# Five taps of each convolution tile on TensorE, and the sink's logit as a score column, in a two-layer decoder trunk

## The chip, the cores and the metric

The kernel runs on one core of one Trainium2 chip. The metric is the device time of one execution in microseconds (us), as a median over several runs. TensorE (PE in the profile) has a clock that is granted at one of two levels, 2.4 or 1.2 GHz; the profile gives it as a share of the higher one.

## The reference

512 tokens of 1024 channels pass two layers and a final RMS norm. The change lies in layer 0's mixer alone. It has two branches over one normalised input:

```python
q, k, v, glu = jnp.split(proj, [A_Q, A_Q + A_KV, A_Q + 2 * A_KV], axis=-1)
a, _ = band_attention(q, k, v, A_WINDOW - 1, sinks)      # 8 heads, window 128
g_a, g_b = jnp.split(glu, 2, axis=-1)
c = g_a * jax.nn.sigmoid(g_b)
c = causal_depthwise_conv(c, conv_w, conv_b)              # 31 taps, 512 channels
c = jax.nn.silu(layer_norm(c, ln_g, ln_b))
return jnp.einsum('bse,ed->bsd', jnp.concatenate([a, c], axis=-1), w_out)
```

In the attention a learned logit per head (the sink) is added to each softmax denominator, with no value behind it:

```python
m = jnp.maximum(jnp.max(s, axis=-1), sink_b)
p = jnp.exp(s - m[..., None])
l = jnp.sum(p, axis=-1) + jnp.exp(sink_b - m)
```

After the mixer stand a SwiGLU layer, layer 1 (dilated attention and a gated unit) and a second SwiGLU layer, all untouched by the change.

## The kernel before

Activations are kept transposed: a tile has 128 channels (or tokens) on the partitions and 512 tokens (or channels) in the free dimension. A product with weights is made of three matmuls on rounded halves (`acc3`, lines 197 to 204: high by high, high by low, low by high); eight of these, over the eight input tiles, make one projection tile. The weights come by DMA in blocks (tile `raw`); ACT rounds them (`w_hi`, L174), and in this stage POOL makes the rest (`w_lo`, L151).

Layer 0's mixer is planned as a list of steps (`C0["steps"]`): `g0` to `g3` are the two projection tiles of one convolution tile each (`a` and `b`), `v`, `k`, `q0` to `q3` the projections of the attention, `S0` to `S3` the scores and `V0` to `V3` the values of two heads each, `A`, `X`, `B`, `Y`, `C` parts of the output projection and `L` the layer norm behind the convolution. TensorE's own order is exactly the order in which the program is written (`manual_schedule`): a planner (`Seq`) counts estimated time, and between two `acc3` it lets the side lines (scores, values, layer norm) put in their matmuls when their planned wait is over. The orders of the other engines are set by a scheduler at build time. Every engine carries out its instructions strictly in its order, so an instruction that waits holds up all behind it.

One convolution tile j has 128 channels. `glu` (L494) makes the padded input `cp` on DVE and ACT. `conv_tile` (L467) splits the 31 taps: ACT makes the scaled copies `prod` (L478; the first one, L475, begins `yc`) and POOL adds them into `yc` (L479); the rest are done by DVE as a chain of multiply-adds in PSUM bank 6 (first tap L481, then L483), and L484 adds the bank to `yc`. Bank 6 is one buffer, so the chains of the four tiles follow each other. `taps=(8, 15, 15, 10)` are the taps of the ACT and POOL part; DVE has 23, 16, 16 and 21. DVE's taps have a low priority (`LATER`), so the scheduler fills them in between other DVE work.

`conv_norm` (L633) turns each finished `yc` on TensorE (L641, into bank 7), takes statistics on DVE (L643) and a copy on ACT (L644); after the fourth tile come the norm (L650 to L662), the turn back (L668) and the activation. `scores0` (L572) makes the scores of two heads in two halves on TensorE (L590, L591); DVE scales, masks and takes the maximum (L598), ACT makes the exponentials and their sums `l` (L610). The sink is treated apart: `es` (L605, L612), its sum with `l` (L614) and the reciprocal (L615). `pt_av` (L399) turns the probabilities (L407, copies `pts` on ACT, L410), multiplies them with the values (L421), scales by the reciprocal on DVE (`on`, L430) and turns the result back (L435). `rope` (L386) is the rotary embedding of q and k.

Of the kernel before, what the change touches and what calls it, by code (L numbers as in the profile page):

```python
# [10 lines left out]
def _warn_once_fixed(msg, *args, **kwargs):  # L11
# [7 lines left out]
F32 = mybir.dt.float32  # L19
# [4 lines left out]
P = 128  # L24
# [18 lines left out]
    taps=(8, 15, 15, 10),  # L43
# [91 lines left out]
def trunk_kernel(ctx: ExitStack, tc: tile.TileContext, xT, ws, cols, sinks, sgu_g, sgu_b,  # L135
# [308 lines left out]
    with ExitStack() as mx:  # L444
# [17 lines left out]
        mp.tile([P, 8, 2 * P], F32, name="Pm", bufs=2)  # L462
# [4 lines left out]
        def conv_tile(j, pool_taps):  # L467

            with tc.high_priority(offset=LATER):
                acc = bank(6)  # L470
                for t in range(TAPS):
# [4 lines left out]
                    elif t < pool_taps:  # L476
                        p = mp.tile([P, S], F32, name="prod", bufs=3)
                        A.activation(p, src, AF.Copy, scale=w)  # L478
                        G.tensor_add(yc[j], yc[j], p)  # L479
                    elif t == pool_taps:  # L480
                        V.tensor_scalar(out=acc, in0=src, scalar1=w, scalar2=None, op0=ALU.mult)  # L481
                    else:
                        V.scalar_tensor_tensor(acc, src, w, acc, op0=ALU.mult, op1=ALU.add)  # L483
                V.tensor_add(yc[j], yc[j], acc)  # L484

# [87 lines left out]
        def scores0(i):  # L573
# [3 lines left out]
            qss = qTs[i][1]  # L577
            Pm = mp.tile([P, 8, 2 * P], F32, name="Pm", bufs=2)
            nm = scr.tile([P, 8], F32, name="nm")
            l = scr.tile([P, 8], F32, name="l")  # L580
            for n2 in range(2):
# [10 lines left out]
                for n1 in range(2):  # L592
                    n = 2 * n2 + n1
                    for b in range(2):
# [4 lines left out]
                            out=Pm[:, u, c0:], in0=sb[b][:, n1 * 256 + c0:n1 * 256 + 256],  # L599
                            in1=mask0[:, c0:], scale=-0.125, scalar=nsink[:, hd:hd + 1],  # L600
                            op0=ALU.add, op1=ALU.min, accum_out=nm[:, u:u + 1])
                if n2 == 0:
                    yield 0.9, C0["S"]
            es = scr.tile([P, 8], F32, name="es")
            V.tensor_tensor(out=es.rearrange("p (n b) -> p n b", b=2),  # L605
                            in0=nm.rearrange("p (n b) -> p n b", b=2),
                            in1=sinkb[:, i:i + 5:4][:, None, :].to_broadcast([P, NQ, 2]), op=ALU.add)
# [4 lines left out]
            A.activation(es, es, AF.Exp)  # L612
            rl = scr.tile([P, 8], F32, name="rl")
            V.tensor_add(rl, l, es)  # L614
            V.reciprocal(rl, rl)  # L615
# [4 lines left out]
        def values0(i):  # L620
# [5 lines left out]
            for u in range(8):  # L626
# [3 lines left out]
                items.append((u, Pm[:, u, P:], n, n == 0, True))  # L630
            yield from pt_av(items, lambda u, blk: Vt[:, blk, 64 * (u % 2):64 * (u % 2) + 64], rl, i, (4, 7))

        def conv_norm():  # L633
# [47 lines left out]
        for step in C0["steps"].split():  # L681
            kind, i = step[0], int(step[1:] or 0)
            if kind == "g":
                pa, pb = gemm_in(f"a{i}"), gemm_in(f"b{i}")

                def after(i=i, pa=pa, pb=pb):
                    glu(i, pa, pb)
                    conv_tile(i, C0["taps"][i])
# [17 lines left out]
            elif kind == "q":  # L706
                ps = gemm_in(step)
                seq.until(lambda: len(qTs) < 2)
                qTs[i] = (mp.tile([P, S], F32, name="qT", bufs=3),
                          [mp.tile([P, S], F32R, name=f"qs{b}", bufs=2) for b in range(2)])  # L710

                def after(i=i, ps=ps, step=step):
                    qT, qss = qTs[i]
# [18 lines left out]
            elif kind == "Y":  # L732
# [4 lines left out]
                early[i] = mp.tile([P, S], F32, name="qT", bufs=3)  # L737
# [603 lines left out]
```

## Time and profile before

| | us |
|---|---|
| median of 3 runs (1117.32, 1123.54, 1124.16) | 1123.54 |
| the profiled execution | 1121.61 |
| its span in the profile | 1119.9 |

The profiled execution's own time is 1.71 us above its span. All durations below come from that one execution. Layer 0's mixer takes the first 208 us of the span; in the first 30 us of them the norm and the first two projection tiles are made. Times in a trace row are from the span's start. A matmul's end is modelled in the records, so the time that a matmul takes of TensorE is read from the distance between starts.

### The profile page before, as it was taken

The numbers are of one execution on the slowest core, as the hardware profiler recorded it, in microseconds if no ns is written. First come the engines' busy times: TensorE is split into PE (matmuls) and PEld (weight loads), VectorE is DVE, ScalarE is ACT, GpSimd is POOL, SyncE is SP. The second block draws the span as 40 slices with busy tenths as digits, with TensorE's granted clock in tenths as the row PEclk, the third lists the DMA queues.
The fourth block names the chain that finished last, engine by engine and source line by source line (L and its number), as shares of the span: only waits on it lengthen the run. The fifth ranks groups of instructions, "written<-read, shape, count | busy, mean of one in ns | idle before, by whom it ended". The sixth has DMA issues, their size and how long they took to land.

```text
span 1119.9 us, 13693 instructions
## 1 busy us (share of the span) xinstructions
PE 1071.8 (96%) x5118; PEld 887.8 (79%) x5118; DVE 693.8 (62%) x1059; ACT 572.9 (51%) x930; POOL 232.8 (21%) x210
## 2 busy tenths in 40 slices
PE   9988789989999999999999999999899999999997
PEld 7767677868788888888887888888688888888785
DVE  3889965777455655654748546666765646555543
ACT  6577756754435343543636654446544453535433
POOL 0789754201101010100014300001111010101002
PEclk9989999999999999999999999999999999999999
DMA  6221112977767677621432111239777676767122
GB/s 230 68 70 57 38 38 75 263 208 190 168 187 150 188 136 217 135 57 50 149 103 76 57 39 58 94 117 237 210 187 179 164 171 180 154 189 150 26 69 76
DMA packets 42803, 145.89 MB, mean 130 GB/s; under 512 B 4848, under 2 KB 5744, under 8 KB 42736
## 3 DMA queue, kind: packets, MB, share of 16 engines
q1 hardware_dynamic: 31072, 102.97, 27.0%
q0 software_dynamic: 11520, 41.95, 22.2%
q8 instruction: 40, 0.66, 0.2%
q14 instruction: 27, 0.22, 0.1%
q10 hardware_dynamic: 144, 0.09, 0.0%
HBM read 142.89 MB, written 2.10 MB: 129 GB/s over the span
## 4 chain that ended last, share of the span: by engine, by line
PE 75%; DVE 9%; DMA 4%; ACT 4%; issue 4%; POOL 3%; POOLq 0%; ACTq 0%; SPq 0%; DVEq 0%
PE bank L201 11%; PE bank L202 10%; PE bank L203 10%; PE bank L904 10%; PE bank L907 10%; PE bank L906 10%; DMA raw<-in_ws 4%; PE bank L262 2%; PE bank L264 2%; PE bank L263 2%; DVE bank L483 2%; PE bank L919 1%; PE bank L421 1%; ACT w2h L880 1%; POOL yc L479 1%
## 5 line engine op out<-in xcount | busy, mean ns | idle before, releaser
L151 DVE TENSOR_TENSOR w2l<-raw,w2h 128x1024 fp32r<-128x1024 f32 x140 | 171.4, 1225 | 206.0 <-ACT w2h L880 206.0
L880 ACT ACTIVATE w2h<-raw 128x1024 fp32r<-128x1024 f32 x140 | 148.0, 1058 | 208.8 <-PE bank L907 159.5
L174 ACT ACTIVATE w_hi<-raw 128x512 fp32r<-128x512 f32 x204 | 127.4, 628 | 180.5 <-PE bank L202 143.4
L870 POOL DMA_DIRECT2D raw<-in_ws x80 | 69.6, 870 | 557.7 <-DVE w2l L151 231.7
L151 DVE TENSOR_TENSOR w_lo<-raw,w_hi 128x512 fp32r<-128x512 f32 x164 | 115.6, 709 | 57.7 <-ACT w_hi L174 57.7
L907 PE MATMUL bank<-w2h,s 128*128 128x512 f32 x320 | 126.0, 394 | 4.3 <-DVE s L151 4.3
L904 PE MATMUL bank<-w2h,s 128*128 128x512 f32 x320 | 126.5, 395 | 2.5 <-ACT s L823 1.4
L906 PE MATMUL bank<-w2l,s 128*128 128x512 f32 x320 | 125.5, 392 | 0.0
L201 PE MATMUL bank<-xh,w_hi 128*128 128x512 f32 x272 | 111.4, 410 | 1.3 <-ACT w_hi L174 1.3
L203 PE MATMUL bank<-xh,w_lo 128*128 128x512 f32 x272 | 108.0, 397 | 0.0
L202 PE MATMUL bank<-xl,w_hi 128*128 128x512 f32 x272 | 107.9, 397 | 0.0
L201 PE MATMUL bank<-hh,w_hi 128*128 128x512 f32 x256 | 100.1, 391 | 1.1 <-DVE hl L151 1.1
L202 PE MATMUL bank<-hl,w_hi 128*128 128x512 f32 x256 | 100.0, 391 | 0.0
L203 PE MATMUL bank<-hh,w_lo 128*128 128x512 f32 x256 | 99.9, 390 | 0.0
L904 PE MATMUL bank<-w2h,xh 128*128 128x512 f32 x240 | 94.4, 393 | 0.0
L907 PE MATMUL bank<-w2h,xl 128*128 128x512 f32 x240 | 93.5, 389 | 0.0
L906 PE MATMUL bank<-w2l,xh 128*128 128x512 f32 x240 | 93.4, 389 | 0.0
L907 PEld LDWEIGHTS bank<-w2h,s 128*128 128x128 f32 x320 | 60.7, 190 | 17.9 <-DVE s L151 5.2
L904 PEld LDWEIGHTS bank<-w2h,s 128*128 128x128 f32 x320 | 60.6, 190 | 16.4 <-ACT s L823 2.3
L906 PEld LDWEIGHTS bank<-w2l,s 128*128 128x128 f32 x320 | 60.5, 189 | 12.4
L151 POOL TENSOR_TENSOR w_lo<-raw,w_hi 128x512 fp32r<-128x512 f32 x40 | 54.6, 1366 | 60.2 <-ACT w_hi L174 57.6
L479 POOL TENSOR_TENSOR yc<-yc,prod 128x512 f32<-128x512 f32 x44 | 60.7, 1381 | 10.5 <-ACT prod L478 9.0
(237 smaller groups left out, 2051.8 us busy)
## 6 DMA issues: line engine op xcount, KB each, us to landing
raw<-in_ws SPq DMA_DIRECT2D x181, 512.0 KB, 4.2
raw<-in_ws POOLq DMA_DIRECT2D x80, 512.0 KB, 5.7
h<-in_xT SPq DMA_DIRECT2D x8, 256.0 KB, 4.8
out_y<-xh SPq DMA_DIRECT2D x4, 256.0 KB, 2.0
out_y<-xl SPq DMA_DIRECT2D x4, 256.0 KB, 2.3
raw<-in_ws SPq DMA_DIRECT2D x2, 256.0 KB, 3.9
ropeC<-in_rope_c SPq DMA_DIRECT2D x2, 256.0 KB, 4.1
ropeS<-in_rope_s SPq DMA_DIRECT2D x2, 256.0 KB, 4.7
```

The lines of the kernel that those rows point to most:

```text
L151: eng.tensor_tensor(out=out, in0=a, in1=b, op=ALU.subtract)
L174: A.activation(hi, src, AF.Copy)
L201: T.matmul(ps, hi, xh, start=start, stop=False)
L202: T.matmul(ps, hi, xl, start=False, stop=False)
L203: T.matmul(ps, lo, xh, start=False, stop=stop)
L262: T.matmul(ps[t], xh[:, c], hi, start=(k == 0), stop=False)
L479: G.tensor_add(yc[j], yc[j], p)
L870: nc.gpsimd.dma_start(t, ws[base + 8 * (g - 1) + 2 * BLOCK_OF[more] + q], accum_op=ALU.add)
L880: A.activation(hi, src, AF.Copy)
L904: T.matmul(ps[t], xh[:, c], wh[:, w], start=(start and j == 0), stop=False, skip_group_check=True)
L906: T.matmul(ps[t], xh[:, c], wl[:, w], start=False, stop=False, skip_group_check=True)
L907: T.matmul(ps[t], xl[:, c], wh[:, w], start=False, stop=(j == 3), skip_group_check=True)
```

## The change

Five taps of each convolution tile leave the chains of ACT, POOL and DVE and become matmuls: ACT scales the identity matrix by a tap's weight column (tile `dg`, a diagonal matrix of 128x128), and TensorE multiplies it with the shifted input `cp`, in float32, five of them accumulated into bank 6. DVE's chain then goes on in that bank with the taps that are left and has no first tap (the former L481) of its own. The taps are now 7, 13, 13, 8 on ACT and POOL, 5, 5, 5, 5 on TensorE and 19, 13, 13, 18 on DVE. The matmuls are a new side line `T` of the planner, with planned times `cv`. The layer norm's planned times `ln` stay, but it does not turn a tile before that tile's five matmuls have been put in.

The scores tile `Pm` gets a 257th column per head and block, which ACT fills with the sink's logit, and the exponential with its sum runs over 257 (or 129) columns. `es`, its exponential and its addition go; the reciprocal is taken from `l`. A q tile's rotary result moves from a tile of its own (`qT`) to the scratch tile `gb`, and the early output sums move to `prod`.

```diff
-    taps=(8, 15, 15, 10),
+    taps=(7, 13, 13, 8), pe_taps=(5, 5, 5, 5),
+    cv=(0.0, 52.0, 67.0, 94.0),
...
-        def conv_tile(j, pool_taps):
+        def conv_tile(j):
             with tc.high_priority(offset=LATER):
-                acc = bank(6)
-                for t in range(TAPS):
+                for t in range(C0["taps"][j]):
...
-                    elif t < pool_taps:
+                    else:
                         p = mp.tile([P, S], F32, name="prod", bufs=3)
                         A.activation(p, src, AF.Copy, scale=w)
                         G.tensor_add(yc[j], yc[j], p)
-                    elif t == pool_taps:
-                        V.tensor_scalar(out=acc, in0=src, scalar1=w, scalar2=None, op0=ALU.mult)
-                    else:
-                        V.scalar_tensor_tensor(acc, src, w, acc, op0=ALU.mult, op1=ALU.add)
+
+        def conv_psum(j):
+            n0, n1 = C0["taps"][j], C0["taps"][j] + C0["pe_taps"][j]
+            yield 0.0, max(1.6, C0["cv"][j] - seq.t)
+            acc = bank(6)
+            for t in range(n0, n1):
+                dg = mp.tile([P, P], F32, name="dg", bufs=6)
+                A.activation(dg, ident, AF.Copy, scale=col("conv_w", j * TAPS + t))
+                T.matmul(acc, dg, cp[j][:, t:t + S], start=(t == n0), stop=(t == n1 - 1))
+            with tc.high_priority(offset=LATER):
+                for t in range(n1, TAPS):
+                    V.scalar_tensor_tensor(acc, cp[j][:, t:t + S], col("conv_w", j * TAPS + t), acc,
+                                           op0=ALU.mult, op1=ALU.add)
                 V.tensor_add(yc[j], yc[j], acc)
+            done.add(("T", j))
+            yield 0.9 * (n1 - n0), 0.0
...
-            Pm = mp.tile([P, 8, 2 * P], F32, name="Pm", bufs=2)
+            Pm = mp.tile([P, 8, 2 * P + 1], F32, name="Pm", bufs=2)
+            A.activation(Pm[:, :, 2 * P:].rearrange("p (n b) o -> p n (b o)", b=2),
+                         nsink[:, i:i + 5:4][:, None, :].to_broadcast([P, NQ, 2]), AF.Copy)
...
-            es = scr.tile([P, 8], F32, name="es")
-            V.tensor_tensor(out=es.rearrange("p (n b) -> p n b", b=2),
-                            in0=nm.rearrange("p (n b) -> p n b", b=2),
-                            in1=sinkb[:, i:i + 5:4][:, None, :].to_broadcast([P, NQ, 2]), op=ALU.add)
...
-            A.activation(es, es, AF.Exp)
             rl = scr.tile([P, 8], F32, name="rl")
-            V.tensor_add(rl, l, es)
-            V.reciprocal(rl, rl)
+            V.reciprocal(rl, l)
...
                 yield 0.0, max(0.0, C0["ln"][j] - seq.t)
+                while ("T", j) not in done:
+                    yield 0.0, 0.3
```

The orders below are those of the built programs. L489 is the new matmul, L492 the taps and L494 the last addition of DVE's chain, L652 the turn of `yc` (L641 before), L436 the turn of `on` (L435 before), L605 and L606 the scores (L590 and L591 before), L613 the masking on DVE (L598 before). Bank names with the same number are one buffer's use.

TensorE, before, where the fourth convolution tile (`yc_139`) is turned: behind the last turn of `on` and eleven `acc3` of the output projection.

```order
L435 MATMUL bank_1509<-ident,on 128x128 x4
L201 MATMUL bank_1516<-oh_312,w_hi 128x512
L202 MATMUL bank_1516<-ol_320,w_hi 128x512
L203 MATMUL bank_1516<-oh_312,w_lo 128x512
...
L201 MATMUL bank_1559<-oh_313,w_hi 128x512
L202 MATMUL bank_1559<-ol_321,w_hi 128x512
L203 MATMUL bank_1559<-oh_313,w_lo 128x512
L641 MATMUL bank_1572<-ident,yc_139 128x128 x4
```

TensorE, now, the same turn: it stands between the third `on` and the two `acc3` behind the fourth tile's five products, ahead of the second half of `S3` (the row with `bank_1480`) and of all of `V3`.

```order
L489 MATMUL bank_1363<-cp_127,dg 128x512 x5
L422 MATMUL bank_1333<-Vt,pts 128x64 x4
L408 MATMUL bank_1402<-ident,Pm 128x128 x2
...
L422 MATMUL bank_1333<-Vt,pts 128x64 x6
...
L204 MATMUL bank_1348<-oh_312,w_lo 128x512
L652 MATMUL bank_1439<-ident,yc_139 128x128 x4
L436 MATMUL bank_1449<-ident,on 128x128 x4
L202 MATMUL bank_1323<-oh_314,w_hi 128x512
L203 MATMUL bank_1323<-ol_322,w_hi 128x512
L204 MATMUL bank_1323<-oh_314,w_lo 128x512
L605 MATMUL bank_1480<-khh_305,qs_1110 128x256
```

The turn moved up, past the last quarter of the scores, the whole of `V3` and nine of the eleven `acc3`.

VectorE, now, the fourth tile's chain (`bank_1363`) from its input `cp_127` to the statistics of its turn:

```order
L514 SCALAR_TENSOR_TENSOR cp_127<-gb,ga 128x512
L492 SCALAR_TENSOR_TENSOR bank_1363<-cp_127,cc,bank_1363 128x512 x3
L613 ISA Pm,nm<-bank_1411,mask_114,nsink 128x128
...
L492 SCALAR_TENSOR_TENSOR bank_1363<-cp_127,cc,bank_1363 128x512
L431 TENSOR_TENSOR on<-bank_1333,rl 128x512
L492 SCALAR_TENSOR_TENSOR bank_1363<-cp_127,cc,bank_1363 128x512 x14
L494 TENSOR_TENSOR yc_139<-yc_139,bank_1363 128x512
L654 BN_STATS bs<-bank_1439 128x6 x4
L661 BN_AGGR mv_1458<-bs 128x2 x4
L663 TENSOR_SCALAR ve_1463<-mv_1458 128x4
```

VectorE, before, the same chain (`bank_1280`), with the first half of `S3` and the second half in the middle of it:

```order
L502 SCALAR_TENSOR_TENSOR cp_127<-gb,ga 128x512
L481 TENSOR_SCALAR bank_1280<-cp_127,cc 128x512
L483 SCALAR_TENSOR_TENSOR bank_1280<-cp_127,cc,bank_1280 128x512 x10
L430 TENSOR_TENSOR on<-bank_1341,rl 128x512
L483 SCALAR_TENSOR_TENSOR bank_1280<-cp_127,cc,bank_1280 128x512 x2
L598 ISA Pm,nm<-bank_1404,mask_114,nsink 128x128
...
L483 SCALAR_TENSOR_TENSOR bank_1280<-cp_127,cc,bank_1280 128x512
L484 TENSOR_TENSOR yc_139<-yc_139,bank_1280 128x512
L430 TENSOR_TENSOR on<-bank_1466,rl 128x512
```

The second half of `S3` and the last `on` moved from inside or right behind the chain to behind the statistics and the norm.

## Rows read from the trace of the kernel before

**Rows 1.** Busy us (x instructions) by stretch: PE, PEld, DVE, ACT, POOL; PEclk, DMA

```profile
30.00:150.00 120.00, 100.69 (x530) 83.37 (x529) 111.73 (x214) 82.84 (x176) 98.28 (x73) 0.96 0.16 53
67.00:68.00 1.00, 0.01 (x1) 0.01 (x1) 0.97 (x2) 1.00 (x1) 1.00 (x2) 0.50 0.00 0
```

**Rows 2.** What TensorE waits for, 33 to 160 us: us in total, times, longest

```profile
PE bank L435 <- DVE on L430: 7.1, 4, 3.5
PE bank L407 <- ACT yn L644: 3.8, 2, 2.8
PE bank L591 <- DVE kl L698: 3.8, 2, 2.5
PE bank L421 <- ACT pts L410: 2.1, 3, 1.3
PE bank L201 <- DVE gb L498: 1.3, 1, 1.3
PE bank L565 <- DVE ga L704: 1.1, 1, 1.1
...
PE bank L590 <- ACT khh L697: 0.5, 1, 0.5
```

**Rows 3.** Groups by line, 30 to 160 us: xcount | busy us, mean ns | idle before

```profile
L483 DVE SCALAR_TENSOR_TENSOR bank<-cp,cc,bank 128x512 f32<-128x512 f32 x72 | 54.1, 751 | 1.2
L598 DVE CUSTOM_DVE_ANT_0 Pm<-bank,mask,nsink 128x256 f32<-128x256 f32 x24 | 10.6, 479 | 0.7 <-PE bank L591 0.7
L605 DVE TENSOR_TENSOR es<-nm,sinkb 128x8 f32<-128x8 f32 x4 | 3.7, 925 | 0.0
L614 DVE TENSOR_TENSOR rl<-l,es 128x8 f32<-128x8 f32 x4 | 2.4, 599 | 0.3 <-ACT es L612 0.3
L610 ACT ACTIVATE Pm<-Pm,nm 128x256 f32<-128x256 f32 x24 | 12.0, 500 | 2.5 <-DVE nm L598 2.5
L479 POOL TENSOR_TENSOR yc<-yc,prod 128x512 f32<-128x512 f32 x44 | 60.7, 1381 | 10.5 <-ACT prod L478 9.0
```

**Rows 4.** TensorE in order of time: start us, us, instruction xcount [idle before <-releaser]

```profile
1.32 4.43 PE L306 MATMUL bank<-sq 128*128 128x256 f32 x10 [1.32 <-DVE sq L303]
29.59 1.05 PE L356 MATMUL bank<-ident,rc 128*128 128x128 f32 x8
30.39 0.48 PE L201 MATMUL bank<-xh,w_hi 128*128 128x512 f32 x1
67.99 0.48 PE L591 MATMUL bank<-kl,qs 128*128 128x128 f32 x1 [2.47 <-DVE kl L698]
69.22 0.63 PE L201 MATMUL bank<-xh,w_hi 128*128 128x512 f32 x1
74.75 0.28 PE L590 MATMUL bank<-khh,qs 128*128 128x256 f32 x1
140.54 0.66 PE L435 MATMUL bank<-ident,on 128*128 128x128 f32 x4 [1.48 <-DVE on L430]
154.10 0.66 PE L435 MATMUL bank<-ident,on 128*128 128x128 f32 x4 [1.24 <-DVE on L430]
208.40 0.95 PE L341 MATMUL bank<-ones,nacc 128*128 128x1 f32 x8
```

**Rows 5.** VectorE in order of time, columns as in rows 4

```profile
34.31 0.68 DVE L502 SCALAR_TENSOR_TENSOR cp<-gb,ga 128x512 f32<-128x512 f32 x1
129.16 0.64 DVE L498 TENSOR_TENSOR gb<-bank,R 128x512 f32<-128x512 f32 x1
132.02 7.88 DVE L483 SCALAR_TENSOR_TENSOR bank<-cp,cc,bank 128x512 f32<-128x512 f32 x10
152.76 0.69 DVE L484 TENSOR_TENSOR yc<-yc,bank 128x512 f32<-128x512 f32 x1
162.80 0.89 DVE L643 BATCH_NORM_STATS2 bs<-bank 128x6 f32<-128x128 f32 x4 [6.68 <-PE bank L641]
166.93 1.87 DVE L659 TENSOR_SCALAR yn<-yn,rs,nmr 128x512 f32<-128x512 f32 x2
```

More of the change, by code (lines that the diff above doesn't have):

```diff
@@ L459, in trunk_kernel @@
         V.tensor_scalar(out=taps, in0=taps, scalar1=0.5, scalar2=None, op0=ALU.mult)
-        mp.tile([P, 8, 2 * P], F32, name="Pm", bufs=2)
+        mp.tile([P, 8, 2 * P + 1], F32, name="Pm", bufs=2)
         for b in range(2):
@@ L576, in scores0 @@
                 yield 0.0, 0.3
-            qss = qTs[i][1]
-            Pm = mp.tile([P, 8, 2 * P], F32, name="Pm", bufs=2)
+            qss = qTs[i]
+            Pm = mp.tile([P, 8, 2 * P + 1], F32, name="Pm", bufs=2)
+            A.activation(Pm[:, :, 2 * P:].rearrange("p (n b) o -> p n (b o)", b=2),
+                         nsink[:, i:i + 5:4][:, None, :].to_broadcast([P, NQ, 2]), AF.Copy)
             nm = scr.tile([P, 8], F32, name="nm")
@@ L598, in scores0 @@
                         V.tensor_tensor_reduce(
-                            out=Pm[:, u, c0:], in0=sb[b][:, n1 * 256 + c0:n1 * 256 + 256],
+                            out=Pm[:, u, c0:2 * P], in0=sb[b][:, n1 * 256 + c0:n1 * 256 + 256],
                             in1=mask0[:, c0:], scale=-0.125, scalar=nsink[:, hd:hd + 1],
@@ L629, in values0 @@
                     items.append((u, Pm[:, u, 0:P], n - 1, True, False))
-                items.append((u, Pm[:, u, P:], n, n == 0, True))
+                items.append((u, Pm[:, u, P:2 * P], n, n == 0, True))
             yield from pt_av(items, lambda u, blk: Vt[:, blk, 64 * (u % 2):64 * (u % 2) + 64], rl, i, (4, 7))
@@ L687, in after @@
                     glu(i, pa, pb)
-                    conv_tile(i, C0["taps"][i])
+                    conv_tile(i)
+                    seq.add("T", conv_psum(i))
             elif kind == "k":
@@ L708, in trunk_kernel @@
                 seq.until(lambda: len(qTs) < 2)
-                qTs[i] = (mp.tile([P, S], F32, name="qT", bufs=3),
-                          [mp.tile([P, S], F32R, name=f"qs{b}", bufs=2) for b in range(2)])
+                qTs[i] = [mp.tile([P, S], F32R, name=f"qs{b}", bufs=2) for b in range(2)]
                 def after(i=i, ps=ps, step=step):
-                    qT, qss = qTs[i]
+                    qT, qss = scr.tile([P, S], F32, name="gb"), qTs[i]
                     rope(ps, qT, tabs, V if step in C0["rope_v"] else G)
@@ L736, in trunk_kernel @@
                     acc3(ps, (oh[k], ol[k]), k == 0, k == 3)
-                early[i] = mp.tile([P, S], F32, name="qT", bufs=3)
+                early[i] = mp.tile([P, S], F32, name="prod", bufs=3)
                 A.activation(early[i], ps, AF.Copy)
```

## The prediction

> **What bounds the kernel now.** I read the stretches first, then what TensorE waits for, then the groups of VectorE, then both engines in order of time. Over the whole span TensorE is nearly always busy, so only what adds to its work or its waits moves the end. The change touches the stretch from 30 to 160 us. There TensorE is busy 100.69 of 120 us and VectorE 111.73: VectorE is the fuller engine, and POOL has 98.28 [rows 1]. The waits say the same: nearly all of TensorE's idle time in this stretch, some 20 us, ends on VectorE or on ACT behind it, above all on `on` (7.1), on the copies of the turned convolution (3.8) and on `kl` (3.8, with 0.5 for `khh` ahead of it) [rows 2]. So a microsecond off VectorE could count here, if it is taken where TensorE waits. From 154.10 to 208.40, on the other hand, TensorE runs through: 74 `acc3` and six turns of four 128-column blocks, and nothing it waits for [rows 4]. Taking 0.4 us for a turn (four of them in the 0.66 us of a row, less its tail), an `acc3` is (54.3 - 2.4) / 74 = 0.70 us, one pass over 512 columns 0.23 us.
>
> **What goes.** VectorE loses 13 taps of the 76 (taps 23, 16, 16, 21 become 19, 13, 13, 18): 13 x 0.75 = 9.8 us, and `es` and its addition, 3.7 + 2.4 = 6.1 us [rows 3]: 15.9 us in all. POOL loses 7 additions of 1.38 us, 9.7 us. ACT loses 7 copies and the small exponentials and gets 20 diagonal matrices of 128x128, each at most the 0.50 us of an exponential of twice that size [rows 3]: 0 to 10 us, and I take the 5 us that go. The first ten are built ahead, so no product waits for them. The 257th column adds one element to rows of 0.50 us: nothing that a row shows. Neither ACT nor POOL sets the end here, so their part counts as nothing; if POOL's relief were needed for `yc` in time, it is there.
>
> **What the products cost.** No row shows a float32 product of 512 columns. From below it is two records of one pass each, 0.46 us; from above twice the 256-column product at the very start, 10 records for five of them in 4.43 us, so 1.77 us. The nearest row is the float32 product with `rc`: four of 128 columns between 29.59 and 30.39, 0.80 us for 512 columns [rows 4]. I take that: 20 x 0.80 = 16.0 us, between 9.2 and 35.4. All of it is on TensorE's path: it stands in TensorE's order, between work that doesn't wait less for it.
> By the Trainium skill ("FP8 and Floating Point Precision", section "TensorE Precision Notes") a true FP32 matmul takes four passes; at 0.23 us each that would be an estimate of 0.93 us a product and 18.6 us in all, 2.6 us more than the sum below has.
>
> **Where VectorE's relief goes.** Before, a tap chain starts as soon as VectorE has made `cp`. Now it waits until TensorE has made five products, which themselves wait for `cp`: 5 x 0.80 = 4.0 us in which VectorE stands idle unless its order has something else. By the order it has nothing else at the first tile (`cp` ends at 35.0 [rows 5]), the third and the fourth, so about 12 of the 15.9 us are given back. The chains' ends come hardly earlier.
> The Trainium skill ("PSUM — Partial Sum Buffer", section "PSUM bank collisions raise a hardware error") has it that two engines in one bank and partitions must be kept apart by semaphores; this speaks against a bank that passes from TensorE to VectorE for each tile. The trace shows such a hand-over as a wait: 1.3 us for VectorE's `gb` to leave a bank [rows 2].
>
> **The sum, along TensorE.** Against before, by place:
> - Products: +16.0.
> - First tile: TensorE stood 1.1 us for `ga` [rows 2]; now it stands until `cp` at 35.0: +0.6.
> - `S0`: TensorE comes 4.6 us later. VectorE's work up to `kl` lost 4 taps, the first tap of the second tile and half a rotary (5.1 us) and got 4.0 us of idle time and some 2 us of waits for projections that come later; `kl` is done about 0.9 us after it was at 67.9. The wait of 2.5 + 1.3 + 0.5 us becomes 0.8: -3.5. The granted clock was 0.50 there [rows 1], and the five `acc3` behind it took 74.75 - 69.22 = 5.5 us [rows 4] where 3.5 are normal. Without the wait the clock stays up: -2.0.
> - `V0`: it now starts one `acc3` and a turn behind the second half of `S0`, so it waits for the fifth exponential, and the copies `pts` stand on ACT behind the copy of the turned first tile: +2.5.
> - `V1`: the turn of the second tile stands 17 `acc3` ahead of it, so the wait of 2.8 us for `yn` goes; the third tile's products wait 1.6 us for their `cp`: -1.2.
> - `V2`: five products stand between its turns and its values, so its 1.3 us for `pts` goes, with an estimated 0.7 of the longest wait for `on`: -2.0. The third `on` is done long before it is turned: -1.5.
> - The fourth tile: behind its products VectorE has 18 taps at 0.79 (7.88 / 10 [rows 5]) = 14.2, four maskings at up to 0.48, `on` and the last addition of 0.7 each: 17.2 us until `yc` is whole. TensorE has in that time 30 records of some 0.10 us (8 in 0.80 [rows 4]) and two `acc3`: 4.5 us. Then it must turn the tile: a new wait of 12.7 us. Before, the tile was whole at 153.4 and turned at 162: nobody waited [rows 5].
> - Behind that turn VectorE does the statistics up to the scaled `yn` (162.80 to 168.80 [rows 5], 6.0 us), 0.7 of `ol`, and only then the second half of `S3`; TensorE needs its fifth exponential, 0.5 + 0.5 us later, at 7.7 us, and has 3.6 us of work: 4.1. The copies wait for the last exponentials: 1.5. Before, 1.2 us stood here: +4.4. The last `on` waits for the activation of the first turned-back tile: +1.4.
> - Where TensorE comes later and VectorE sets the pace, part of TensorE's added work is covered: the switches of its own and half of the small waits at the first two `on`: an estimate of -4.0 from their 0.9 + 3.5 us.
> Together 16.0 + 0.6 - 5.5 + 2.5 - 1.2 - 3.5 + 12.7 + 4.4 + 1.4 - 4.0 = +23.4 us. The profiled execution took 1121.61 us, 1.9 below the median of the runs, so the forecast is 1121.6 + 23.4 = 1145 us. Everything from 208.40 on (the same instructions in the same order on all engines) only moves.
> A check from the other side: what stood behind the third `on` at 140.54 [rows 4] is now pinned to the fourth tile's end. Before, it began 11.4 us after the fourth tile's projection was free (129.16 [rows 5]); now it begins after 2.4 us to `cp`, some 1 us more until the products, 4.0 of products and 17.2 of the chain, 24.6 us. That is 13 us later, whatever happened until 129, and before the 5.8 us at its end.
>
> **Rivals.**
> 1. Faster: VectorE's relief decides. If its 15.9 us come through, the seven waits of rows 2 go, 19.7 us, and the slow clock's 2.0; with a product near its lower bound, at 0.50 us, 10.0 and the 0.6 stand against that: 1121.6 - 11.1 = 1110 us. It decides where the fourth tile is whole when TensorE comes to turn it. For it: VectorE is the fullest engine and all these waits end on it. Against it: the fourth turn would have to find its tile whole 4.5 us after the products, with 18 taps to go. Chance 0.08.
> 2. About equal: the relief comes through, but the fourth tile's wait stands. If the scheduler's order covers VectorE's idle time at the starts of the chains, the fourth tile comes up to 12 us earlier, and with products at 0.60 us another 4 go: 23.4 - 16 = +7.4, 1129 us. For it: the product's price is unknown downwards. Against it: the order shows no other VectorE work at three of the four starts. Chance 0.17.
> 3. Slower still: a product costs 1.77 us. Then 19.4 us more, 1164 us; from 1.2 us on it leaves the range. For it: only the rows of the first 5 us of the span, of a TensorE that had done nothing before. Chance 0.05.
> The clock may also fall in the new wait of 12.7 us, as it stood at 0.50 in the wait before 67.99 [rows 1, 4]; what then runs at the lower level costs some 2 us, as there, and lies in the forecast's own range. The Trainium skill ("TensorE: Matmul & The Clock Gate", section "HAM oscillation — how this bites in real kernels") says so too: idle gaps send the array back to the lower clock.
>
> **How the numbers follow.** The forecast has 0.70, with a range of its own of 1135 to 1155: 10 us below for products at 0.46 us (-6.8) and a smaller `V0`, 10 above for the clock and products of 1.2 us (+8). The range reaches down to 1124 to take in rival 2, and leaves out rivals 1 and 3. A measurement of this kernel can tell about 1% from no change, 11.2 us around 1123.5: faster 0.08, same 0.17 and slower 0.70 + 0.05.
>
> **What would show it.** In the changed kernel's profile the matmuls with `dg` start 0.8 us apart; TensorE's longest wait is the turn of `yc` for VectorE's last addition, over 10 us at about 146; the wait for `kl` is under 1.5 us and the clock is 1.00 at 67; VectorE is idle about 4 us ahead of the first taps of tiles one, three and four; the sum of squares that begins at 208.40 [rows 4] begins at about 230. I am wrong if that turn waits under 5 us, if VectorE's chains start right behind `cp`, or if the mixer ends before 215.

## The result, and the profile after

The changed kernel takes 1161.92 us (median of 4 runs, 1159.69 to 1163.86); the kernel before, run beside it, 1121.71. The ratio is 1.0358, 95% interval 1.0328 to 1.0389: slower, as forecast, but by more than the range allowed (1145, 1124 to 1155). The profiled execution took 1159.69 us, with a span of 1157.9, 38.0 us more than before.

The sum of squares that began at 208.40 [rows 4] begins at 236.48. So 28.1 us were lost in layer 0's mixer, and 9.9 us behind it, where no instruction is new and TensorE's order is the same: from this sum to the end it took 911.5 us before and 921.4 after.

First the stretches (columns as in rows 1; the third is that of the new wait):

```profile
30.00:150.00 120.00, 107.53 (x530) 84.03 (x529) 86.71 (x167) 77.59 (x165) 85.36 (x64) 0.97 0.17 53
67.00:68.00 1.00, 1.00 (x6) 0.84 (x5) 1.00 (x1) 0.97 (x2) 1.00 (x2) 1.00 0.02 8
155.00:175.00 20.00, 8.02 (x30) 5.95 (x30) 13.45 (x34) 4.78 (x13) 1.03 (x1) 0.57 0.00 0
```

From 30 to 150 us VectorE is busy 86.71 us where it had 111.73 [rows 1], TensorE 107.53 instead of 100.69. VectorE is no longer the fuller engine in this stretch; a part of its work now comes later than 150, so the difference is not what it was relieved of. Around 67 TensorE now works at full clock. In the 20 us from 155 it works 8.02.

What TensorE waits for, 30 to 250 us (us in total, times, longest), to be set against rows 2:

```profile
PE bank L652 <- DVE yc L494: 12.2, 1, 12.2
PE bank L408 <- ACT yn L655: 5.9, 1, 5.9
PE bank L436 <- DVE on L431: 5.4, 2, 2.9
PE bank L489 <- DVE cp L514: 2.1, 2, 1.7
PE bank L436 <- ACT yn L655: 1.6, 1, 1.6
PE bank L422 <- ACT pts L411: 1.4, 3, 0.7
PE bank L202 <- DVE gb L510: 0.9, 1, 0.9
```

`kl` and `khh` have gone from the list. The first row is the new wait at the turn of the fourth convolution tile (L652). The second stands at the first turn of `Pm`, in `V0`. The slow clock of the kernel before around 67 has not simply gone: behind the wait in `V0` the granted clock is 0.50, where it was 1.00 before the change. First the changed kernel, then the kernel before:

```profile
82.00:88.00 6.00, 4.45 (x19) 4.17 (x20) 4.43 (x9) 3.94 (x10) 4.37 (x4) 0.50 0.01 3
```

```profile
82.00:88.00 6.00, 4.87 (x35) 4.24 (x36) 5.93 (x18) 4.39 (x10) 4.32 (x4) 1.00 0.00 0
```

TensorE in order of time (columns as in rows 4):

```profile
68.13 0.22 PE L605 MATMUL bank<-khh,qs 128*128 128x128 f32 x1
...
71.11 4.45 PE L489 MATMUL bank<-cp,dg 128*128 128x512 f32 x10
...
83.55 1.97 PE L408 MATMUL bank<-ident,Pm 128*128 128x128 f32 x8 [5.88 <-ACT yn L655]
...
142.59 4.46 PE L489 MATMUL bank<-cp,dg 128*128 128x512 f32 x10
146.89 1.00 PE L422 MATMUL bank<-Vt,pts 128*128 128x64 f32 x8
...
163.93 1.09 PE L652 MATMUL bank<-ident,yc 128*128 128x128 f32 x4 [12.17 <-DVE yc L494]
166.63 1.12 PE L436 MATMUL bank<-ident,on 128*128 128x128 f32 x4 [1.61 <-ACT yn L655]
...
182.75 0.63 PE L436 MATMUL bank<-ident,on 128*128 128x128 f32 x4 [2.59 <-DVE on L431]
```

Five products are ten records, and the next instruction starts 146.89 - 142.59 = 4.30 us behind the first: 0.86 us a product, 17.2 us for twenty. The four turns of `on` begin at 93.4, 127.6, 166.6 and 182.7; before, at 87.5, 117.0, 140.5 and 154.1.

VectorE, at the start of the first and the third chain and from the fourth `cp` to the fourth tile's last addition:

```profile
40.03 1.55 DVE L492 SCALAR_TENSOR_TENSOR bank<-cp,cc,bank 128x512 f32<-128x512 f32 x2 [4.78 <-PE bank L489]
...
107.23 3.13 DVE L492 SCALAR_TENSOR_TENSOR bank<-cp,cc,bank 128x512 f32<-128x512 f32 x4 [4.65 <-PE bank L489]
...
139.51 0.92 DVE L514 SCALAR_TENSOR_TENSOR cp<-gb,ga 128x512 f32<-128x512 f32 x1 [0.70 <-ACT gb L512]
147.09 2.34 DVE L492 SCALAR_TENSOR_TENSOR bank<-cp,cc,bank 128x512 f32<-128x512 f32 x3 [6.65 <-PE bank L489]
...
151.95 11.04 DVE L492 SCALAR_TENSOR_TENSOR bank<-cp,cc,bank 128x512 f32<-128x512 f32 x14
163.09 0.69 DVE L494 TENSOR_TENSOR yc<-yc,bank 128x512 f32<-128x512 f32 x1
```

In brackets stands the idle time: VectorE waits 4.78, 4.65 and 6.65 us, 16.1 in all, for products before it can go on in their bank. That is as much as it was relieved of. Its taps in the whole mixer now, and below them the four first taps of the kernel before (columns as in rows 3):

```profile
L492 DVE SCALAR_TENSOR_TENSOR bank<-cp,cc,bank 128x512 f32<-128x512 f32 x63 | 47.5, 754 | 17.6 <-PE bank L489 16.1
```

```profile
L481 DVE TENSOR_SCALAR bank<-cp,cc 128x512 f32<-128x512 f32 x4 | 3.0, 748 | 0.2
```

Before, the taps took 54.1 [rows 3] + 3.0 us, now 47.5. With `es` and its addition, 3.7 + 2.4 us [rows 3], VectorE lost 15.7 us of work.

The 9.9 us behind the mixer show in the starts of matmuls that follow each other without a gap. In the feed-forward part of the changed kernel:

```profile
453.87 0.39 PE L918 MATMUL bank<-w2h,s 128*128 128x512 f32 x1
454.10 0.39 PE L915 MATMUL bank<-w2h,s 128*128 128x512 f32 x1
454.32 0.39 PE L917 MATMUL bank<-w2l,s 128*128 128x512 f32 x1
454.55 0.39 PE L918 MATMUL bank<-w2h,s 128*128 128x512 f32 x1
454.78 0.40 PE L202 MATMUL bank<-hh,w_hi 128*128 128x512 f32 x1
...
455.48 0.39 PE L202 MATMUL bank<-hh,w_hi 128*128 128x512 f32 x1
...
456.18 0.40 PE L202 MATMUL bank<-hh,w_hi 128*128 128x512 f32 x1
```

Four `w2h,s` and `w2l,s` start in 454.78 - 453.87 = 0.91 us, 227 ns apart. The six from there to 456.18 (with two others between each shown) are 233 ns apart, at the same granted clock. Before the change, both kinds were 227 ns apart.

### The profile page after: what moved, and what is told of

Read it like the earlier page. It is cut to its first block, busy times and chain, and to the rows that moved or that the text cites. A ratio compares the mean times of both kernels' runs of the same rounds, so it can differ in the third digit from the quotient of the medians.

```text
span 1157.9 us, 13768 instructions
## 1 busy us (share of the span) xinstructions
PE 1100.9 (95%) x5158; PEld 896.5 (77%) x5158; DVE 679.9 (59%) x1038; ACT 574.7 (50%) x943; POOL 222.5 (19%) x203
## 3 DMA queue, kind: packets, MB, share of 16 engines
q0 software_dynamic: 11520, 41.95, 21.6%
## 4 chain that ended last, share of the span: by engine, by line
PE 79%; DVE 8%; ACT 5%; DMA 3%; issue 3%; POOL 1%; SPq 0%; POOLq 0%; ACTq 0%; DVEq 0%
PE bank L202 11%; PE bank L203 11%; PE bank L204 11%; PE bank L915 10%; PE bank L918 10%; PE bank L917 10%; DMA raw<-in_ws 3%; PE bank L263 2%; PE bank L265 2%; PE bank L264 2%; DVE bank L492 2%; PE bank L422 2%; PE bank L930 1%; PE bank L489 1%; PE bank L408 1%
## 5 line engine op out<-in xcount | busy, mean ns | idle before, releaser
L152 POOL TENSOR_TENSOR w_lo<-raw,w_hi 128x512 fp32r<-128x512 f32 x40 | 54.1, 1352 | 87.9 <-ACT w_hi L175 87.9
L917 PEld LDWEIGHTS bank<-w2l,s 128*128 128x128 f32 x320 | 60.5, 189 | 12.7
L945 DVE TENSOR_TENSOR h<-h,bank 128x512 f32<-128x512 f32 x69 | 47.1, 685 | 27.2 <-PE bank L204 27.2
```

Source lines behind the costliest of these rows:

```text
L152: eng.tensor_tensor(out=out, in0=a, in1=b, op=ALU.subtract)
L917: T.matmul(ps[t], xh[:, c], wl[:, w], start=False, stop=False, skip_group_check=True)
L945: V.tensor_add(h[n], h[n], ps)
```

## Experiments

Two things were open: what the mixer's 28.1 us are made of, and where the 9.9 us come from. The start of the sum of squares behind the mixer ("the sum") separates them. Ratios are to the kernel before, run beside each.

**One part alone.** e1 is the kernel before with the column (the rest of it, the fill by ACT and the widths of the slices, is as in the change):

```diff
-        mp.tile([P, 8, 2 * P], F32, name="Pm", bufs=2)
+        mp.tile([P, 8, 2 * P + 1], F32, name="Pm", bufs=2)
...
-            es = scr.tile([P, 8], F32, name="es")
...
-            V.tensor_add(rl, l, es)
-            V.reciprocal(rl, rl)
+            V.reciprocal(rl, l)
```

> The kernel before with the score column for the sink alone; the convolution stays as it was. Theory A (the place of the fourth tile's turn and the products cost the mixer its 28.1 us, the column nothing): the sum of squares behind the mixer begins at 205 to 209 us (208.40 before), since VectorE loses 6.1 us of `es` work and only waits for `on` can get shorter. Rival R (the column has a price, on ACT's exponentials or as a wait for its fill): it begins at 211 or later. The 9.9 us that were lost behind the mixer, where 512-column matmuls stood 233 ns apart in stretches instead of 227: theory P (they go with where the tiles lie in memory, which the column and the dropped `es` move by 64 bytes) says that they are here too, so in all +6 to +10 us, ratio 1.005 to 1.009. Theory Q (they go with the five products or with the one execution) says 227 ns here and a ratio of 0.995 to 1.001.

1135.42 us, ratio 1.0117 (1.0081 to 1.0154), with the sum at 209.6, of which 1.8 us were lost ahead of the changed stretch (the product with `rc` begins at 31.4 instead of 29.6): nothing lost in the mixer. Behind it stand 925.5 us instead of 911.5. A single profile is not sharp there: with the tiles of the later layers where they lay before, this stretch takes 908.3 (e11) to 914.4 us (e8); with the 64 bytes gone, 921.4 (changed) to 925.5 (e1). e2 is the changed kernel with `es` as before:

```diff
+            es = scr.tile([P, 8], F32, name="es")
...
-            V.reciprocal(rl, l)
+            V.tensor_add(rl, l, es)
+            V.reciprocal(rl, rl)
```

> The changed kernel with the sink as before (es, its exponential, its addition, 256 columns); only the five products per tile, and the moved tiles that make room. Theory A: the mixer loses as much as with the whole change or a few us more, since VectorE keeps 6.1 us of `es` work: the sum of squares begins at 236 to 242 us, with one wait of 11 to 16 us at the fourth tile's turn. Rival: the column alone set the fourth tile's delay, and it begins under 225. Theory P (place in memory): all tiles of the later layers lie where they lay before, so 512-column matmuls stand 227 ns apart there and the end comes 28 to 34 us later than before, no more than the mixer lost: ratio 1.025 to 1.031. Theory Q with the products as cause: 233 ns here too, and a ratio of 1.034 to 1.040.

Ratio 1.0271 (1.0240 to 1.0302), 1152.33 us, the sum at 239.1, the wait at the fourth turn 12.2 again, 911.8 us behind it. So the mixer's loss belongs to the products and the time behind it to the column or what goes with it. The kernel before once more:

> The kernel before once more, for the distance of its matmuls behind the mixer on the chip on which the other three run. Theory P: 227 ns, the same as in its first profile. If it is 233 here, the 9.9 us belong to the chip or the execution and not to the kernel.

1120.99 us (one execution), the sum at 208.2, then 911.1 us, 227 ns: it is no matter of the chip.

**The place of tiles in memory.** Without `es`, two scratch tiles of 32 bytes a partition are gone, and everything allocated later lies 64 bytes lower. e5, e6 and e7 change places alone, by a tile that nothing uses (here two buffers of 32 bytes; e7 has two of 64):

```diff
             l = scr.tile([P, 8], F32, name="l")
+            scr.tile([P, 8], F32, name="pad")
```

> The changed kernel with an unused scratch tile of 64 bytes in place of the two of 32 bytes that `es` had: every tile of the later layers lies again where it lay before the change, all instructions stay. Theory P (a 512-column matmul is slow where its moving and its stationary operand lie differently within 128 bytes of a partition): 227 ns again between matmuls behind the mixer, the stretch from the sum of squares behind the mixer to the end takes 911 to 913 us as before instead of 921.4, and the whole kernel about 1151.5 us, ratio to the kernel before 1.025 to 1.030. Rival (dropping the `es` instructions did it, by another order on some engine): 921 us, ratio 1.034 to 1.039.

1151.30 us, ratio 1.0271 (1.0252 to 1.0289); behind the sum 912.5 us. The same instructions in the same place as before cost what they cost before. The mixer is as slow as in the changed kernel, with the sum at 237.2.

> The kernel before with an unused scratch tile of 64 bytes, nothing else: the tiles of the later layers lie 64 bytes further. Theory P: they stand at 32 within 128 bytes where the input tiles stay at 96, so matmuls of the one with the other go to 233 ns, and the kernel is 10 to 14 us slower, ratio 1.008 to 1.013. Rival: no difference, 0.997 to 1.003.

Ratio 1.0063 (1.0041 to 1.0085): slower, by less than expected; the matmuls concerned stand 229 ns apart and not 233.

> The same with 128 bytes. Theory P: the place within 128 bytes is as before, 227 ns, ratio 0.997 to 1.003. If any shift does it (or it is the place within a larger unit), it is slower as with 64 bytes, ratio 1.008 to 1.013.

Ratio 1.0080 (1.0061 to 1.0098). Here the theory fell in its first form: 128 bytes are not the unit. e8 is e1 with the 64 bytes.

> The score column for the sink alone (the first experiment) with the unused 64 bytes. Theory P: the 14 us of that experiment go, 1120 to 1124 us, ratio 0.997 to 1.003; the column itself then is worth nothing that can be measured, or up to 3 us of gain from the shorter waits for `on`. Rival (the column costs by itself): ratio 1.008 to 1.015 as without the 64 bytes.

1122.32 us, ratio 0.9996 (0.9975 to 1.0018): the 13 us of e1 were the place alone, and the column is worth nothing that can be measured.

For all pairs of 512-column matmuls that follow each other at full clock, the distance of their starts in the trace was then set beside the addresses in the built program: address of the moving operand minus that of the stationary one, modulo 256 bytes. Pairs in which it differs between the two matmuls are left out. Each entry is the mean of its pairs.

```
ns apart (number of pairs)
difference             0              64             128            192
before             227.1 (3712)   229.3 (170)
changed            228.0 (1776)   229.1 (354)                    233.4 (1709)
e6, shift  64      227.5 (1764)   229.1 (1715)   232.3 (170)     233.3 (185)
e7, shift 128      227.9 (1751)                  232.5 (1897)    233.3 (170)
e13, shift 256     227.1 (3710)   229.4 (170)
e14, shift 192     228.0 (1937)   229.1 (185)                    233.4 (1710)
e17, hh, hl, s     227.5 (1765)   229.6 (1242)                   233.3 (824)
```

Before, `hh` lay at 168800 and `w_hi` at 79200, 350 times 256 apart; after, `hh` lay at 168736. The rule was made from the first four lines; the other three are its tests, with tiles of 256 and 192 bytes:

> The kernel before with an unused scratch tile of 256 bytes. Theory P256 (the difference of the two operands' places within 256 bytes sets the distance): the later layers are at difference 0 again, 227 ns, ratio 0.997 to 1.003. Rival (any shift from the first layout costs, or the unit is larger): 1.006 or more.

Ratio 0.9998 (0.9972 to 1.0024), 227.1 ns.

> The same with 192 bytes, which is the changed kernel's shift of -64 within 256. Theory P256: 233.4 ns for the products of shifted with unshifted tiles, as in the changed kernel, and 1.008 to 1.012, more than at 64 bytes (1.006) and at least as much as at 128 (1.008). Rival (it grows with the distance, without a period, or 64 and 192 are alike): 1.005 or less, or 229 ns.

Ratio 1.0101 (1.0060 to 1.0142), 233.4 ns. And one that moves a part of the tiles of the feed-forward part, so that the rule asks for other slow products than those of the changed kernel:

```diff
             del homes
+            fp.tile([P, 48], F32, name="pad")
```

> The kernel before with an unused tile of 192 bytes in the feed-forward pool behind w2h and w2l, ahead of hh, hl and s. Theory P256 (own operands): products of hh, hl, s with w_hi, w_lo at difference 192 go to 233.4 ns (864 of them), products of w2h, w2l with s at 64 to 229 ns (960, and 192 more at the end), products of w2h, w2l with xh, xl, slow in the changed kernel, stay at 227 ns. 864 x 6.3 + 1152 x 2.0 = 7.7 us, ratio 1.004 to 1.010. Rival (some other tile's place, a buffer of DMA or of the rounding, sets it): the products with xh slow too, or all at 227 ns and a ratio of 0.997 to 1.003.

Ratio 1.0062 (1.0040 to 1.0084); behind the mixer `hh` with `w_hi` 233.2 ns, `w2h` with `s` 229.9, `w2h` with `xh` 227.5 (233.4 in the changed kernel). So the two operands of a matmul set it, and not the place of one tile. Whether the operands of the matmul that follows take part is not settled: of the pairs left out of the table, those that go from difference 0 to 192 stand 226.3 ns apart in the changed kernel (33 pairs, `w2h,s` ahead of `hh,w_hi`), as the first matmul's own difference asks, but those that go from 0 to 128 in e7 stand 232.6 ns apart (33 pairs of the same kind).

**The fourth turn.**

```diff
-    ... ln=(54.8, 69.91, 96.75, 112.86),
+    ... ln=(54.8, 69.91, 96.75, 128.0),
```

> The changed kernel with the fourth convolution tile turned where it was before the change, behind the last turn of `on` and 11 acc3 (its planned time 128 instead of 112.86); all else the same. Theory A: the wait of 12.2 us goes, with the slow clock behind it, the second half of S3 comes at once, and the layer norm is again covered by the output projection: the sum of squares begins at 214 to 219 us instead of 236.5, ratio to the kernel before 1.014 to 1.020 if the 9.9 us behind the mixer stay, which they should by theory P (same place in memory as the changed kernel). Rival C (VectorE is late anyway, and the last `on` or the norm's copies wait in its place): it begins at 226 or later, ratio over 1.025.

Ratio 1.0222 (1.0191 to 1.0253), the sum at 223.8. What TensorE waits for, 30 to 250 us, in e3:

```profile
PE bank L408 <- ACT yn L655: 5.9, 1, 5.9
PE bank L436 <- DVE on L431: 4.0, 3, 2.9
PE bank L422 <- ACT pts L411: 2.3, 3, 1.5
...
PE bank L489 <- DVE cp L514: 2.1, 2, 1.7
```

The row of 12.2 is gone and 12.7 us came back: the wait and no more. That is 5 us short of theory A (219 at the latest) and clear of rival C (226 or later). In the stretch from 155 to 175 the granted clock was still 0.74, with no wait over 1.6 us in it (columns as in rows 1):

```profile
155.00:175.00 20.00, 17.26 (x81) 14.79 (x82) 12.55 (x25) 6.48 (x16) 2.63 (x3) 0.74 0.08 27
```

It fell to 0.50 between 162 and 163 us, while TensorE carried out the turns and products of `V3`, and was back at 1.00 at 173, in the output projection. e9 has all four turns where they were before, and the 64 bytes:

```diff
-    ... ln=(54.8, 69.91, 96.75, 112.86),
+    ... ln=(62.6, 83.0, 113.3, 128.0),
```

> The changed kernel with the unused 64 bytes and with all four convolution tiles turned where they were before the change (behind the same matmuls of scores, values and acc3). Theory A (what the mixer lost beyond the products is the place of the turns): the 5.9 us at the first tile go as the 12.2 at the fourth did, the sum of squares behind the mixer begins at 216 to 219 us instead of 237.2 (223.8 with the fourth turn alone), ratio 1.007 to 1.010. Rival (VectorE's idle time at the starts of the chains is what delays the values; the wait at the first tile only moves to the exponentials or to `on`): 221 us or later, ratio 1.012 or more.

Ratio 1.0146 (1.0112 to 1.0180), the sum at 226.6: a miss for theory A and what the rival said, 2.8 us later in the mixer than with the fourth turn alone. TensorE's waits in e9:

```profile
PE bank L436 <- DVE on L431: 5.1, 3, 3.9
PE bank L489 <- DVE cp L514: 4.1, 2, 2.4
PE bank L408 <- ACT Pm L622: 2.6, 2, 2.4
PE bank L408 <- ACT yn L656: 2.4, 2, 1.6
```

The 5.9 us are gone from their place and stand in others, for VectorE or for ACT: these four rows have 14.2 us, the four of e3 14.3. The first `on` is turned at 93.4 as before the move, so the bank of the turned tile alone does not hold up `V0`. The granted clock is 0.50 from 82 to 91 here too. In all the mixer loses 18.2 us in e9, not much more than the 17.2 of its products.

**The products' share.** In e10 (on e9) and e11 (on e5) four of five products are left out:

```diff
-                T.matmul(acc, dg, cp[j][:, t:t + S], start=(t == n0), stop=(t == n1 - 1))
+                if t == n1 - 1:
+                    T.matmul(acc, dg, cp[j][:, t:t + S], start=True, stop=True)
```

> The one above with one product per tile in place of five: four taps of each tile are left out of the convolution, so this is a time only. TensorE loses 16 products of 0.88 us, 14.1 us; VectorE's chains keep their length and start up to 3.5 us earlier. Theory A (products stand on TensorE's path whole): the sum of squares begins 11 to 14 us earlier than above. Rival (VectorE sets the pace of the mixer, the products lie beside its work): 6 us or less.

Ratio 1.0017 (0.9995 to 1.0038), the sum at 209.5, 17.0 us earlier than in e9 for 16 x 0.86 = 13.8 us of products: more than theory A said (11 to 14). e10 was also late by 1.5 us when its first product began (36.8 against 35.3), so the edit itself is worth 18.5. Where the last 4.7 us come from is not shown; VectorE's chains begin earlier, too.

> The same on the changed kernel with the 64 bytes and its own turns (1151.3 us): one product per tile, four taps of each tile left out. Theory A as in the prediction's sum: the fourth tile's turn still waits for VectorE's last addition, and what is ahead of it loses the products of three tiles (12 x 0.88) and 3.5 us at the fourth, 14 us in all less what VectorE covers: 10 to 14 us, 1137 to 1141 us. Rival (the chains' own length sets the fourth tile's end): 6 us or less, 1145 or later.

1137.17 us, 14.1 less than e5. In the profiles the third `on` comes 10.4 us earlier and the sum 9.2, but this execution, too, was 1.6 us late when its first product began (36.9 against 35.3): the edit is worth 12.0 at the third `on` and 10.8 at the sum, of 13.8 us of products. Those of the fourth tile count although its turn still waits 11.7 us for VectorE, since VectorE's chain begins behind them. The fourth tile in e5:

```profile
142.67 4.46 PE L489 MATMUL bank<-cp,dg 128*128 128x512 f32 x10
...
164.00 1.09 PE L653 MATMUL bank<-ident,yc 128*128 128x128 f32 x4 [12.15 <-DVE yc L494]
```

and in e11:

```profile
135.51 1.02 PE L490 MATMUL bank<-cp,dg 128*128 128x512 f32 x2
...
153.61 1.09 PE L654 MATMUL bank<-ident,yc 128*128 128x128 f32 x4 [11.66 <-DVE yc L495]
```

From the first product to the turn it is 21.3 us in e5 and 18.1 in e11. So with products for all four tiles they cost most of their time or all of it.

**The clock in the wait.** e15 is e5 with work in the wait:

```diff
+                for k in range(46 if j == 3 else 0):
+                    T.matmul(pt, xs[k % KT][0][:, :P], xs[k % KT][0], start=True, stop=True)
```

> The changed kernel with the unused 64 bytes, and with 46 matmuls of 512 columns, whose results are overwritten, in TensorE's wait at the fourth tile's turn (46 x 0.227 = 10.4 of the 12.2 us). Theory K (the clock that falls in the wait costs the 9.8 us behind it half their speed, some 4.9 us): the granted clock stays at 1.00 from 150 to 175, the sum of squares begins at 231 to 234 us instead of 237.2, 1145 to 1148 us in all, ratio 1.021 to 1.025. Rival (VectorE and ACT set the pace behind the turn, the clock costs nothing): 236 us or later, 1150 to 1153 us.

1150.18 us, ratio 1.0260 (1.0211 to 1.0310), the sum at 237.5. Its stretches around the turn, which begins at 165.03 (columns as in rows 1):

```profile
155.00:165.00 10.00, 8.40 (x38) 6.61 (x36) 9.48 (x13) 0.00 (x0) 0.00 (x0) 1.00 0.00 0
165.00:175.00 10.00, 7.14 (x25) 5.41 (x26) 5.05 (x21) 4.11 (x11) 1.03 (x1) 0.55 0.01 2
```

The clock stays up in the wait and falls right behind it, to 0.55 in a stretch in which TensorE is busy 7.14 of 10 us. Holding it in the wait brought nothing, as the rival said; what the fall behind the turn costs stays open.

**The start of V0.** VectorE's order has two copies for the second q tile ahead of the second half of `S0`'s maskings; e16 (on e5) puts the second tile's products behind that half, and the maskings come first:

```diff
-    cv=(0.0, 52.0, 67.0, 94.0),
+    cv=(0.0, 54.0, 67.0, 94.0),
```

> The changed kernel with the unused 64 bytes and the second tile's five products behind the second half of S0 in TensorE's order, not ahead of it (planned time 54 in place of 52). By the order VectorE then masks that half ahead of the two copies for the second q tile. Theory M (these copies, which wait for POOL and ACT, hold up the maskings, the exponentials and V0): TensorE's wait of 5.9 us at V0 falls under 2, the first `on` is turned at 87 to 90 us instead of 93.5, the sum of squares behind the mixer begins at 232 to 235 instead of 237.2, in all 1146 to 1149 us, ratio 1.022 to 1.026. Rival (the 5.9 us only move to the next place that waits for VectorE, and the fourth tile's chain is as late as it was): the first `on` earlier, but the sum of squares at 236 or later.

Ratio 1.0224 (1.0196 to 1.0252), 1148.46 us, 2.8 less than e5. The wait falls to 4.6, not under 2, and the sum comes at 236.3, as the rival had it, but in an execution whose `S0` began 1.6 us later than e5's. The copies are a part of it at most; the rest of the 5.9 us stays open.

**Versions meant to keep what is good.** e12 has products for two tiles alone (`taps=(8, 15, 13, 8), pe_taps=(0, 0, 5, 5)`, with the 64 bytes of e9 and planned times `cv` and `ln` of its own):

> A version meant to keep what is good: the sink's column, the 64 bytes, the turns where they were, and products for the third and fourth tile alone (the first two as before the change). Theory A: the first two tiles go as before with the shorter waits for `on` of the column alone (2 to 3 us ahead); the ten products cost 8.8 us and bring back up to 7 us, since VectorE's 8 taps fewer shorten the waits for the later `on`: the sum of squares begins at 207 to 213 us, ratio 0.997 to 1.004. Rival (each product costs its full time, whatever the tile): 215 to 218 us, ratio 1.006 to 1.009.

Ratio 1.0039 (1.0018 to 1.0060), the sum at 211.9. Against e8, which has the same column and the same 64 bytes and its sum at 207.9, the ten products (8.6 us by 0.86 each) cost 4.0 us: with six taps, some 4.5 us, taken off VectorE, about half of their time came back here. e18 is e8 with a second unused tile of 128 bytes in the mixer's pool:

> The score column for the sink alone with two unused tiles (64 bytes in the scratch pool, 128 in the mixer's) that put all pairs of operands of 512-column matmuls at difference 0, those of the mixer's output projection too (192 products at 229.3 ns in the kernel before). Theory P256: 227 ns everywhere, 0.4 us from these products, and 0 to 3 us from VectorE's shorter work up to the third `on`: ratio 0.996 to 1.000. Rival: the column's gain is lost in slow clock stretches or waits of the output projection, 1.000 to 1.003.

Ratio 0.9987 (0.9968 to 1.0005). All pairs are at difference 0 and 227.1 ns; the version is not to be told from the kernel before. Nothing that ran is measurably faster than it.

## Why the prediction was wrong, and where it was right

**The step that failed** is "Everything from 208.40 on (the same instructions in the same order on all engines) only moves." The instructions did stay; their tiles moved by 64 bytes when `es` went. In the changed kernel 1709 pairs were 233.4 ns apart instead of 227.1: 10.8 us, where the stretch took 9.9 more. e5 gives it back, e14 brings it about in the kernel before. The prediction had costed "the 257th column" and `es` by their instructions alone. Without this the profiled execution would have been at 1121.6 + 28.1 = 1149.7 us, within the forecast's own range; e5 measured 1151.30.

**The mixer**, +23.4 forecast, +28.1 measured. At the places of the mixer in order, the forecast added up from its steps and without the -4.0 of its last one:

| | forecast | measured |
|---|---|---|
| first scores | +4.6 | +4.7 |
| first `on` | +5.6 | +5.9 |
| second `on` | +8.4 | +10.6 |
| third `on`, behind the fourth tile's turn | +21.6 | +26.1 |
| last `on` | +27.4 | +28.6 |
| the sum of squares | +27.4, with the cover +23.4 | +28.1 |

- "12.7" at the fourth tile: 12.2 waited, 12.7 given back by e3. Its parts too: VectorE needs 163.78 - 147.09 = 16.7 us for the chain, where 17.2 were forecast. This term and its place were right.
- "16.0" for the products: 17.2, at 0.86 us each. The estimate by the four passes of the Trainium skill ("FP8 and Floating Point Precision", section "TensorE Precision Notes") was 0.93; the 0.86 measured lies between it and the 0.80 of the sum.
- `S0`: the wait for `kl` is gone and the clock is at 1.00, as said. But the "-2.0" for the clock did not last: the clock is at 0.50 in `V0` instead (82 to 88 us), which the sum did not have.
- `V0`, "+2.5": the wait is 5.9, with the slow clock behind it. The second half of `S0` ahead of it begins at 75.0 as before (74.75), five products later and two `acc3` fewer. So the first `on` is right by its sum and not by its parts.
- "cover -4.0" and the small gains of `V1`, `V2` and the third `on` were too large together: all terms but the products and the 12.7 add up to -5.3 in the forecast, and to 28.1 - 12.7 - 17.2 = -1.8 in the trace. At `V1` the wait for `yn` did go; which of the others failed is not taken apart here. VectorE lost 15.7 us of work (15.9 forecast) and stood 16.1 us ahead of its chains (some 12 forecast); TensorE was left with a gain of 1.8, net of the new waits.
- Behind the fourth turn "+4.4" and "+1.4" were too large: from the third `on` to the sum 2.0 us were lost. There a wait of 1.6 for the copy `yn`, which was not forecast, comes ahead of the third `on`.

Together 23.4 + 1.2 (products) + 3.5 (gains that did not come) + 9.9 (behind the mixer) = 38.0.

**The signs named.** Products 0.8 us apart: 0.86. The longest wait at the turn of `yc`, over 10 us: yes, from 151.8 on, not 146. The wait for `kl` under 1.5 us and the clock at 1.00 at 67: both. VectorE idle ahead of the chains: 4.8, 4.7 and 6.7 us at the first, third and fourth tile. The sum at about 230: 236.5. None of the three signs of being wrong came; none of them looked behind the mixer.

**The rivals.** VectorE's relief does not decide (1), even where the turn is moved away (e3, e9). Nor was its idle time at the chains' starts covered, as (2) needed: it stood 16.1 us there. A product at 1.77 us (3) did not come, though its time, 1164 us, was nearest: right size, wrong cause. Of the clock the forecast had "some 2 us"; the clock was at 0.57 from 155 to 175, but e15 shows no gain from holding it up in the wait. That it falls in an idle gap agrees with the Trainium skill ("TensorE: Matmul & The Clock Gate", section "HAM oscillation — how this bites in real kernels").

## What to carry to other kernels

When an edit adds, drops or resizes a tile, compare the addresses of all tiles behind it before and after. In this kernel of some 4100 matmuls of 512 columns, 64 bytes cost 13 us with the column alone (e1), whose own work was worth nothing that could be measured, and 10 us in the changed kernel. An unused tile of 64 bytes gave them back both times (e8, e5). Where one engine carries the path, work taken off another engine pays only at a wait that the path really has, and work put on the path has to be counted: twenty products cost most of their time or all of it here (e10, e11), ten of them, where they relieved a busy VectorE, about half (e12). When a producer ends later, look where an in-order engine stands waiting for it: moving the fourth turn behind the later end brought 12.7 us back (e3), moving the other three as well brought nothing (e9).

## What was unexpected in the hardware

- The distance of 512-column matmuls on rounded halves depends on where the moving operand lies relative to the stationary one within 256 bytes of a partition: 227 ns at 0, 229 at 64, 232.5 at 128, 233.4 at 192, as means over the pairs, to within 1 ns in each of the seven layouts of the table. Other differences, and why it is so, were not tried. The Trainium skill ("SBUF — State Buffer", section "Operand start alignment") has a rule on where an operand may start and says that it is about legality and that nothing was timed; all addresses here keep it.
- A float32 product of 512 columns is two records of 0.43 us, 0.86 us in all.
- In e3 the granted clock averaged 0.74 from 155 to 175 us with TensorE busy 17.26 of 20 us. It fell between 162 and 163, while TensorE carried out turns of 128 and products of 64 columns, behind a wait of 1.5 us, and came back at 173 in a row of 512-column matmuls.
